# Attention of a decoder trunk: pairs of heads run in common slots, heads side by side in row tiles

## The chip, the cores and the metric

One core of a Trainium2 chip runs the whole kernel. The metric is the device time of one execution, in microseconds; a median stands for the runs shown.

## The reference, cut to what matters

One layer of a decoder trunk on 256 tokens of width 1024, in fp32: a feed-forward with a norm, a mixer with a norm, a second feed-forward with a norm. The mixer runs three causal attentions of six heads each (head width 64) and adds them through sigmoid gates:

```python
x = LN(alpha*x + 0.5*SwiGLU_a(x))
h = x @ w_in                      # q, k, v of three branches, and gates
# MoBA: with 256 tokens and blocks of 256 only the query's own block is left
p = softmax(where(dist >= 0, q k^T / 8 - slope*dist, -inf));  o_m = p v
# differential: two maps of width 32 for each head
w = softmax(s_1) - lam*softmax(s_2);  o = w v
o_d = o * rsqrt(mean(o^2) + eps) * subln_g * (1 - lambda_init)
# stick-breaking: strictly causal
z = q k^T / 8;  log_1m = where(before, log_sigmoid(-z), 0)
tail = cumsum(log_1m, reverse) - log_1m
o_s = where(before, exp(log_sigmoid(z) + tail), 0) v
x = LN(alpha*x + (sum_b sigmoid(g_b + c_b) * (o_b w_br_b)) @ w_out)
x = LN(alpha*x + 0.5*SwiGLU_b(x))
```

## The kernel before

**Big products.** Every weight chunk (128 x 1024) is loaded raw by SP's queue, and then split into a high part, by ACT (L113), and the rest, by DVE (L114), both float32r. A product is made of three: high by high, high by rest, rest by high. `nat_mm` holds the activations and moves 512 weight columns; `trn_mm` holds weight columns and moves 512 and then 256 token columns. Nine split tiles rotate (`HL_BUFS`), and three more where there is room. Products add up in the four PSUM banks of the pool `acc`; the four of `att` serve attention and transposes.

**The order.** The schedule is written by the program itself. Class `Pe` keeps a clock of its own, moved on by each recorded matmul; `pe.later(delay, fn)` queues a piece, and before each product's matmul the pieces that have come due are recorded. So a piece of attention stands wherever that clock reached its time, among the matmuls of a big product, and its ACT and DVE instructions stand at the same place in those engines' rows. `MIX` lists the mixer's products: queries and keys of a pair of heads (`project`), gates in halves (`gates`), branch products (`branch`). Pairs of heads start at least `PACE` = 10 of that clock apart, stick-breaking first (three pairs), then differential, then MoBA.

**Attention of a pair** is in plain fp32, both token tiles at once: 128 columns for the first (only its own keys) and 256 for the second.
- MoBA: `softmax_scores` of each head (two matmuls with 64 rows, at row 0 or 64 of the array); on DVE the bias, the mask and the row's extreme (L574), on ACT the exponential with its sum (L577); `MB_T` later six transposes and two copies on ACT (L585); `MB_O` later `pv` (six matmuls with the transposed map held and 64 value columns moving), a division by the sums on DVE, and `O_M` later `turn_o`, two transposes into `oT`, the form that the branch product needs.
- Differential: two maps of 32 rows for each head. The first head's two maps, then `D_H` later the second's; the combination (L652 to L655) `D_C` after each, the transposes `D_T` after, `pv` at `D_O`, a norm of the output, `turn_o` at `D_F`.
- Stick-breaking: for each head a matmul that writes the mask to a bank over the whole array (`identr` held, `maskr` moving, 384 columns), then the scores onto it (64 rows, heads at row 0 and 64). ACT and DVE make a softplus (L706 to L709) and split it. `ST_T` later the sums (a triangular matrix by both parts) and the carry (`mones`), and an exponential on ACT (L724); `ST_O` later the values, with V held and the map moving, which gives the transposed output at once.

L186 is the one line of all matmuls (`Pe.mm`), L190 that of the transposes (`Pe.tr`).

Of the kernel before, what the change touches and what calls it, by code (L numbers as in the profile page):

```python
# [10 lines left out]
F32 = mybir.dt.float32  # L11
# [5 lines left out]
P = 128  # L17
# [14 lines left out]
# split weight chunks and raw ones held at a time; the first chunks split before the products begin  # L32
# [14 lines left out]
# distances between dependent pieces on TensorE's queue: between pairs of heads, then of the norms' transposes  # L47
# (T), the hidden units' (N), MoBA (MB, O), differential (D) and stick-breaking (ST)
# [102 lines left out]
class Pe:  # L151
    """Matrix products in program order, with a clock by which later pieces are slotted in."""
# [42 lines left out]
def trunk(ctx: ExitStack, tc: tile.TileContext, start_d, x_d, ln_g, ln_b, gu_d, gun_d, down_d, v_d, qk_d, gate_d,  # L195
# [48 lines left out]
    with ExitStack() as es:  # L244
# [10 lines left out]
        # TensorE's clock comes up while the first pieces load  # L255
# [121 lines left out]
    def to_T(src, dst, t, q):  # L377
        """Four 128-column pieces of src (token tile t) transposed and split into dst."""
# [8 lines left out]
    def nat_mm(ps, lhs, k, t, h, l, lo, n, first, last):  # L387
        """One k tile: activations (token tile t) stationary, n weight columns from lo moving."""
# [6 lines left out]
    def trn_mm(ps, src, h, l, k, first, last):  # L395
        """One k tile: 128 weight columns stationary; hi products left, the rest right."""
# [136 lines left out]
    with ExitStack() as es:  # L533
# [6 lines left out]
        # values: the first token tile of two branches first, while the second is normalised  # L540
# [39 lines left out]
        def turn_rows(e):  # L580
# [3 lines left out]
            eT = ep.tile([P, BW], F32, name="eT", bufs=3)  # L584
# [3 lines left out]
        def pv(ps, eT, b, h, r):  # L588
            vc = vcol(b, h)
            o0, o1 = ps[:, r * HD:(r + 1) * HD], ps[:, P + r * HD:P + (r + 1) * HD]  # L590
            pe.mm(o0, eT[:, 0:P], V[:, 0, vc], True, True)
            pe.mm(o1, eT[:, P:S], V[:, 0, vc], True, False)
            pe.mm(o1, eT[:, S:BW], V[:, 1, vc], False, True)

        def turn_o(o, b, p):
            ps = att.tile([P, 512], F32, name="att")
            for t in range(2):
                pe.tr(ps[:, t * P:(t + 1) * P], o[:, t * P:(t + 1) * P], ident)
            act_split(oT[b][:, p, 0:S], oT[b][:, p, S:2 * S], ps[:, 0:S])
            pairs_done[b] += 1  # L600
# [3 lines left out]

        def moba_pair(p, qT, kT):
            sm = small.tile([P, 2, 2], F32, name="sm")
            nmx = small.tile([P, 2, 2], F32, name="nmx")
            es_ = []
            for r in range(2):
                e = ep.tile([P, BW], F32, name="e")  # L610
                softmax_scores(qT, kT, r * 64, 64, SLOPES[2 * (2 * p + r)], e, nmx[:, r, :], sm[:, r, :])
                es_.append(e)
            exps[0] -= 1
            eTs = []

            def values():
                eTs.extend(turn_rows(e) for e in es_)

            def more():
                ps = att.tile([P, 512], F32, name="att")  # L620
                for r in range(2):
                    pv(ps, eTs[r], 0, 2 * p + r, r)
                rs = small.tile([P, 2, 2], F32, name="rsm")
                nc.vector.reciprocal(rs, sm)
                o = ep.tile([P, S], F32, name="s1", bufs=5)
                nc.vector.tensor_tensor(
                    o.rearrange("p (t r c) -> p t r c", t=2, r=2),
                    ps[:, 0:S].rearrange("p (t r c) -> p t r c", t=2, r=2),
                    rs.rearrange("p r t -> p t r").unsqueeze(3).to_broadcast([P, 2, 2, HD]), op=ALU.mult)
                pe.later(O_M, lambda: turn_o(o, 0, p))  # L630
            pe.later(MB_T, values)
            pe.later(MB_O, more)

        def diff_pair(p, qT, kT):
            sm = small.tile([P, 2, 2, 2], F32, name="smd")
            nmx = small.tile([P, 2, 2, 2], F32, name="nmxd")
            ws_ = {}
            eTs = {}

            def head(r):  # L640
                sl = SLOPES[2 * (2 * p + r) + 1]
                ee = []
                for m in range(2):
                    e = ep.tile([P, BW], F32, name="e")
                    softmax_scores(qT, kT, r * 64 + m * 32, 32, sl, e, nmx[:, m, r, :], sm[:, m, r, :])
                    ee.append(e)
                if r:
                    exps[0] -= 1

                def combine():  # L650
                    c = small.tile([P, 2], F32, name="c")
                    nc.vector.reciprocal(c, sm[:, 1, r, :])  # L652
                    nc.vector.scalar_tensor_tensor(c, sm[:, 0, r, :], nlam, c, op0=ALU.mult, op1=ALU.mult)
                    for t, cs in enumerate((slice(0, P), slice(P, BW))):
                        nc.vector.scalar_tensor_tensor(ee[0][:, cs], ee[1][:, cs], c[:, t:t + 1], ee[0][:, cs],  # L655
                                                       op0=ALU.mult, op1=ALU.add)
                    ws_[r] = ee[0]

                def turn():
                    eTs[r] = turn_rows(ws_[r])  # L660
                pe.later(D_C, combine)
                pe.later(D_T, turn)

            def more():
                ps = att.tile([P, 512], F32, name="att")
                for r in range(2):
                    pv(ps, eTs[r], 1, 2 * p + r, r)
                rs = small.tile([P, 2, 2], F32, name="rsm")
                nc.vector.reciprocal(rs, sm[:, 0])
                o = ep.tile([P, S], F32, name="s1", bufs=5)  # L670
# [4 lines left out]
                sq = ep.tile([P, S], F32, name="s1", bufs=5)  # L675
# [5 lines left out]
                nc.gpsimd.tensor_tensor(ms, ms, mhalf[:, 0:4], op=ALU.pow)  # L681

# [5 lines left out]
                pe.later(D_F, lambda: turn_o(o, 1, p))  # L688
            head(0)
            pe.later(D_H, lambda: head(1))  # L690
            pe.later(D_O, more)

        def stick_pair(p, qT, kT):
            zs, sps = [], []
            sh = lnp.tile([P, D], F32R, name="ln_g")
            sl = lnp.tile([P, D], F32R, name="ln_b")
            for r in range(2):
                ps = att.tile([P, 512], F32, name="att")
                rr = slice(r * 64, (r + 1) * 64)
                pe.mm(ps[:, 0:BW], identr, maskr, True, False, skip_group_check=True)  # L700
                pe.mm(ps[:, 0:S], kT[rr, 0:P], qT[rr, 0:S], False, False, tile_position=(r * 64, 0),
                      skip_group_check=True)
# [205 lines left out]
```

## Time and profile before

| | |
|---|---|
| median of 3 runs | 616.0 us (612.36, 616.0, 618.33) |
| span of the profiled execution | 612.6 us |
| mean granted clock of TensorE | 0.997 |
| busy: PE, weight loads | 601.5, 511.3 us |
| busy: DVE, ACT, GpSimd | 406.5, 327.6, 26.9 us |

The profiled execution's span is that from its first to its last instruction; no other time of that execution is given, and the fastest of the three runs is 612.36 us. The mixer with its attention lies between about 223 and 400 us; attention ends at 352.

### The profile page before, as it was taken

How to read it: one execution, taken by the hardware profiler on the slowest of the kernel's cores; microseconds unless marked ns; L12 is line 12 of the kernel's file. 1: busy time of each engine (PE TensorE's matmuls, PEld its weight loads, DVE VectorE, ACT ScalarE, POOL GpSimd, SP SyncE). 2: the span in 40 equal slices, each digit the busy share in tenths (PEclk: the TensorE clock that was granted, in tenths of full speed). 3: DMA queues.
4: the chain of work that ended last, by engine and by line, in shares of the span. 5: the costliest groups of instructions: out<-in, count | busy, mean ns of one | idle time of the engine just before them, and what ended most of it. 6: DMA issues, size and time to landing. Idle time of an engine off the chain costs nothing.

```text
span 612.6 us, 8640 instructions
## 1 busy us (share of the span) xinstructions
PE 601.5 (98%) x3186; PEld 511.3 (83%) x3186; DVE 406.5 (66%) x656; ACT 327.6 (53%) x561; POOL 26.9 (4%) x63
## 2 busy tenths in 40 slices
PE   8999999999999999999999999999999999999995
PEld 7888888888889988878688888888788888888884
DVE  5879767664438666567786586789866676674217
ACT  6868556553312677565647564444755566563200
POOL 1610000000001000000020000001000000000001
PEclk9999999999999999999999999999999999999998
DMA  8899765666531783443444547454965566656001
GB/s 326 288 365 311 261 180 180 191 194 210 155 103 61 259 307 122 150 154 119 139 143 157 173 171 239 138 172 163 321 239 196 185 183 193 201 185 197 1 1 68
DMA packets 32538, 113.35 MB, mean 185 GB/s; under 512 B 3680, under 2 KB 4448, under 8 KB 32496
## 3 DMA queue, kind: packets, MB, share of 16 engines
q1 hardware_dynamic: 30816, 106.97, 52.6%
q0 software_dynamic: 1680, 5.83, 3.0%
q8 instruction: 25, 0.41, 0.3%
q14 instruction: 17, 0.14, 0.1%
HBM read 111.74 MB, written 1.05 MB: 184 GB/s over the span
## 4 chain that ended last, share of the span: by engine, by line
PE 89%; DVE 3%; issue 3%; DMA 3%; ACT 1%; POOL 0%; SPq 0%; DVEq 0%; ACTq 0%; POOLq 0%
PE acc L186 82%; PE att L186 6%; DMA raw<-gu 2%; PE att L190 1%; DMA sraw<-start 1%; DVE wx L114 1%; DVE w L114 1%; ACT wx L113 0%; POOL rs L353 0%; DVE x L362 0%; ACT e L577 0%; DVE x L358 0%; DVE e L574 0%; DVE e L655 0%; ACT w L113 0%
## 5 line engine op out<-in xcount | busy, mean ns | idle before, releaser
L114 DVE TENSOR_TENSOR w<-raw,w 128x1024 fp32r<-128x1024 f32 (+1 forms) x166 | 197.8, 1206 | 76.8 <-ACT w L113 76.0
L186 PE MATMUL acc<-xT,w 128*128 128x512 f32 x1264 | 228.1, 339 | 0.0
L186 PEld LDWEIGHTS acc<-xT,w 128*128 128x128 f32 x1264 | 193.7, 188 | 29.2 <-issue 1.5
L113 ACT ACTIVATE w<-raw 128x1024 fp32r<-128x1024 f32 (+1 forms) x166 | 170.5, 1040 | 83.0 <-PE acc L186 70.4
L186 PE MATMUL acc<-w,xT 128*128 128x512 f32 (+1 forms) x576 | 132.5, 382 | 0.0
L186 PEld LDWEIGHTS acc<-w,xT 128*128 128x128 f32 x576 | 104.4, 188 | 17.0 <-issue 1.0
L186 PE MATMUL acc<-w,hT 128*128 128x512 f32 (+1 forms) x408 | 93.5, 383 | 0.0
L186 PEld LDWEIGHTS acc<-w,hT 128*128 128x128 f32 x408 | 74.9, 188 | 14.9
L465 ACT ACTIVATE lo<-acc 128x256 f32<-128x256 f32 x76 | 27.9, 375 | 60.0 <-PE acc L186 60.0
L467 DVE TENSOR_TENSOR gu<-acc,lo 128x256 f32<-128x256 f32 x76 | 31.3, 419 | 38.7 <-ACT lo L465 38.6
L114 DVE TENSOR_TENSOR wx<-raw,wx 128x1024 fp32r<-128x1024 f32 (+1 forms) x30 | 36.3, 1212 | 12.7 <-ACT wx L113 12.6
L186 PE MATMUL acc<-xT,wx 128*128 128x512 f32 x240 | 43.9, 337 | 0.0
L186 PEld LDWEIGHTS acc<-xT,wx 128*128 128x128 f32 x240 | 36.7, 188 | 5.2
L113 ACT ACTIVATE wx<-raw 128x1024 fp32r<-128x1024 f32 (+1 forms) x30 | 31.3, 1046 | 11.5 <-PE acc L186 10.2
L186 PE MATMUL acc<-wx,hT 128*128 128x512 f32 (+1 forms) x138 | 32.8, 380 | 0.0
L186 PEld LDWEIGHTS acc<-wx,hT 128*128 128x128 f32 x138 | 25.2, 188 | 4.9
L344 DVE SCALAR_TENSOR_TENSOR x<-x,acc 128x512 f32<-128x512 f32 x11 | 7.5, 682 | 28.1 <-PE acc L186 28.1
L186 PE MATMUL acc<-w,oT 128*128 128x512 f32 x108 | 25.6, 392 | 0.0
L353 POOL TENSOR_TENSOR rs<-rs,mhalf 128x1 f32<-128x1 f32 x6 | 5.9, 976 | 406.6 <-DVE rs L352 406.6
L240 ACT ACTIVATE hT<-gu 128x256 fp32r<-128x256 f32 x40 | 16.6, 415 | 13.1 <-DVE gu L472 12.1
L186 PEld LDWEIGHTS acc<-w,oT 128*128 128x128 f32 x108 | 20.1, 188 | 4.0
L471 ACT ACTIVATE gu<-gu 128x256 f32<-128x256 f32 x40 | 16.4, 409 | 2.6 <-DVE gu L467 2.5
(132 smaller groups left out, 411.4 us busy)
## 6 DMA issues: line engine op xcount, KB each, us to landing
raw<-gu SPq DMA_DIRECT2D x76, 512.0 KB, 4.9
raw<-down SPq DMA_DIRECT2D x44, 512.0 KB, 4.1
raw<-gates SPq DMA_DIRECT2D x24, 512.0 KB, 4.2
raw<-qk SPq DMA_DIRECT2D x18, 512.0 KB, 4.4
raw<-v SPq DMA_DIRECT2D x12, 384.0 KB, 3.1
raw<-w_out SPq DMA_DIRECT2D x8, 512.0 KB, 5.1
raw<-gun SPq DMA_DIRECT2D x8, 512.0 KB, 4.9
sraw<-start SPq DMA_DIRECT2D x7, 384.0 KB, 6.1
```

Source lines behind the costliest of these rows:

```text
L113: self.nc.scalar.activation(h[:, :n], raw[:, :n], AF.Copy)
L114: self.nc.vector.tensor_tensor(l[:, :n], raw[:, :n], hv[:, :n], op=ALU.subtract)
L186: self.nc.tensor.matmul(out, lhsT=lhsT, rhs=rhs, start=start, stop=stop, **kw)
L190: self.nc.tensor.transpose(out, in_, ident)
L240: nc.scalar.activation(dst_h, src, AF.Copy)
L344: nc.vector.scalar_tensor_tensor(xs, xs, ALPHA, ps[:, 0:n], op0=ALU.mult, op1=ALU.add)
L353: nc.gpsimd.tensor_tensor(rs, rs, mhalf[:, 0:1], op=ALU.pow)
L465: nc.scalar.activation(lo, ps[:, S:2 * S], AF.Copy)
L467: nc.vector.tensor_tensor(v, ps[:, 0:S], lo, op=ALU.add)
L471: nc.scalar.activation(g, g, AF.Silu)
```

## The change

All pairs that are under way advance together. A pair is now a list of stages, each a table from a kind of piece to a function, and `slot()` takes the next stage of every pair, and runs all pieces of one kind before those of the next, in the order `KINDS`. A new pair enters with each slot, and slots are `PACE` apart. Besides that:
- `scores` records the scores of both heads of a pair, or of the differential pair's four maps, kind by kind, so that neighbours stand in different row tiles. The four maps take two banks from `acc` and two from `att`. Stick's two masks come together, before both heads' scores.
- MoBA normalises the rows of its map on DVE (`M_N` after the scores) ahead of the transposes, and then takes `values_T`, with V held, in place of `pv` and `turn_o`.
- The two combinations of a differential pair come 5 and 7 after the scores (`D_C0`, `D_C1`). The pool of `s1` has 3 tiles for 5, that of `eT` 4 for 3, and a tile `o` is new.

Comments and docstrings go, which shifts line numbers: L186, L190, L113, L114, L574, L577, L585, L655, L724 are L180, L184, L106, L107, L582, L585, L593, L663, L745 after.

```diff
-MB_T = 4.0
-MB_O = 6.0
-O_M = 2.5
-D_H = 4.0
-D_C = 3.5
-D_T = 8.0
-D_O = 14.0
+M_N = 4.0
+D_C0 = 5.0
+D_C1 = 7.0
 D_S = 2.5
-D_F = 7.0
-ST_T = 6.5
-ST_O = 1.5
...
-    def mm(self, out, lhsT, rhs, start, stop, **kw):
+    def mm(self, out, lhsT, rhs, start, stop, share=1, **kw):
...
-        self.t += (n / 2.4 if r else max(4 * n / 2.4, 214)) / 1000
+        self.t += (n / 2.4 if r else max(4 * n / 2.4, 214)) / share / 1000
...
-        def softmax_scores(qT, kT, r0, kk, slope, e, nmx, sm):
-            ps = att.tile([P, 512], F32, name="att")
-            r = slice(r0, r0 + kk)
-            tp = (r0, 0)
-            pe.mm(ps[:, 0:P], qT[r, 0:P], kT[r, 0:P], True, True, tile_position=tp)
-            pe.mm(ps[:, P:BW], qT[r, P:S], kT[r, 0:S], True, True, tile_position=tp)
+        def scores(maps, qT, kT, row_q):
+            st, mv = (qT, kT) if row_q else (kT, qT)
+            first = row_q
+            for kind in range(2):
+                for r0, n, ps in maps:
+                    r, tp = slice(r0, r0 + n), (r0, 0)
...
+                    pe.mm(out, st[r, a], mv[r, b_], first, first, tile_position=tp, share=len(maps),
+                          skip_group_check=not row_q)
...
+        def values_T(b, p, eTs):
+            po = att.tile([P, 512], F32, name="att")
+            for kt, cs, ws in ((0, slice(0, S), slice(0, S)), (1, slice(P, S), slice(S, BW))):
+                for r in range(2):
+                    pe.mm(po[r * HD:(r + 1) * HD, cs], V[:, kt, vcol(b, 2 * p + r)], eTs[r][:, ws], kt == 0, kt == 1,
+                          tile_position=(0, r * 64), share=2, skip_group_check=True)
+            act_split(oT[b][:, p, 0:S], oT[b][:, p, S:2 * S], po[:, 0:S])
             pairs_done[b] += 1
...
+        KINDS = ("sums", "mask", "carry", "turn_o", "pv", "turn", "valT", "scores")
...
+                def norm():
+                    rs = small.tile([P, 2, 2], F32, name="rsm")
+                    nc.vector.reciprocal(rs, sm)
+                    for r in range(2):
+                        for t, cs in enumerate((slice(0, P), slice(P, BW))):
+                            nc.vector.tensor_scalar(es_[r][:, cs], es_[r][:, cs], rs[:, r, t:t + 1], None,
+                                                    op0=ALU.mult)
+                pe.later(M_N, norm)
+
+            return [{"scores": start},
+                    {"turn": lambda: eTs.extend(turn_rows(e) for e in es_)},
+                    {"valT": lambda: values_T(0, p, eTs)}]
...
+                banks = [(acc if i < 2 else att).tile([P, 512], F32, name="acc" if i < 2 else "att")
+                         for i in range(4)]
+                scores([(i * 32, 32, banks[i]) for i in range(4)], qT, kT, True)
...
+                pe.later(D_C0, lambda: combine(0))
+                pe.later(D_C1, lambda: combine(1))
...
+            return [{"scores": start},
+                    {"turn": lambda: eTs.extend(turn_rows(e) for e in ee[::2])},
+                    {"pv": pv},
+                    {"turn_o": turn_o}]
...
+            return [{"mask": mask, "scores": start},
+                    {"sums": sums, "carry": carry},
+                    {"valT": lambda: values_T(2, p, wts)}]
...
+        def slot(new=None):
+            if new is not None:
+                under_way.append(new)
+                begun[0] += 1
+            now = [pair.pop(0) for pair in under_way]
+            for kind in KINDS:
+                for stage in now:
+                    if kind in stage:
+                        stage[kind]()
+            under_way[:] = [pair for pair in under_way if pair]
+            if begun[0] == 3 * NP and under_way:
+                pe.later(PACE, slot)
...
-            def begin():
-                begun[0] += 1
-                attend[b](p, *res)
-            pe.later(at - pe.t, begin)
+            pe.later(at - pe.t, lambda: slot(attend[b](p, *res)))
```

**Where the instructions move.** On PE, the first stick-breaking pair (slot one), inside the next pair's query product: the masks (`maskr`) and the scores (`qT,kT`) of two heads, before.

```order
778 L186 MATMUL att<-maskr,identr 128x384
779 L186 MATMUL att<-qT,kT 128x256
780 L186 MATMUL att<-qT,kT 128x128
781 L186 MATMUL att<-maskr,identr 128x384
782 L186 MATMUL att<-qT,kT 128x256
783 L186 MATMUL att<-qT,kT 128x128
784 L186 MATMUL acc<-xT,w 128x256
```

The same place after:

```order
777 L180 MATMUL acc<-xT,w 128x512
778 L180 MATMUL att<-maskr,identr 128x384 x2
779 L180 MATMUL att<-qT,kT 128x256 x2
780 L180 MATMUL att<-qT,kT 128x128 x2
781 L180 MATMUL acc<-xT,w 128x256
```

The second head's mask no longer stands between the two heads' scores, and both heads' matmuls of one shape are neighbours.

On PE, the first differential pair's scores (`kT,qT`) in a gate product, before: two maps of the first head, the third stick pair's values (`eT,V`), a big product's piece (`acc<-w,xT`), then two maps of the second head, of which the last row is cut off here.

```order
917 L186 MATMUL att<-kT,qT 128x128
918 L186 MATMUL att<-kT,qT 128x256
919 L186 MATMUL att<-kT,qT 128x128
920 L186 MATMUL att<-kT,qT 128x256
921 L186 MATMUL att<-eT,V 64x256
922 L186 MATMUL att<-eT,V 64x128
923 L186 MATMUL att<-eT,V 64x256
924 L186 MATMUL att<-eT,V 64x128
925 L186 MATMUL acc<-w,xT 128x512 x13
926 L186 MATMUL att<-kT,qT 128x128
927 L186 MATMUL att<-kT,qT 128x256
928 L186 MATMUL att<-kT,qT 128x128
```

After, slot four, where the first differential pair starts together with the second stick pair's values (`eT,V`) and the third's sums:

```order
893 L180 MATMUL att<-ln_g,trir 128x384
894 L180 MATMUL att<-ln_b,trir 128x384
895 L180 MATMUL att<-e,mones 128x128 x2
896 L180 MATMUL att<-eT,V 64x256 x2
897 L180 MATMUL att<-eT,V 64x128 x2
898 L180 MATMUL acc<-kT,qT 128x128 x2
899 L180 MATMUL att<-kT,qT 128x128 x2
900 L180 MATMUL acc<-kT,qT 128x256 x2
901 L180 MATMUL att<-kT,qT 128x256 x2
902 L180 MATMUL acc<-w,xT 128x512 x32
```

Four maps stand side by side, two of them in banks of `acc`, and pieces of three pairs form one stretch between two pieces of a big product.

On DVE, between the scores of slot five (the second differential pair's) and the transposes of slot six, after: weight splits (`w<-raw,w`) and the combinations (L659 to L663, reading `c`) of that pair's two heads.

```order
241 L787 SCALAR_TENSOR_TENSOR qT<-acc,qsc,s_2812 128x256
242 L790 TENSOR_TENSOR kT<-acc,s_2833 128x256
243 L107 TENSOR_TENSOR w<-raw,w 128x1024 x2
244 L659 RECIPROCAL c<-smd 128x2
245 L660 SCALAR_TENSOR_TENSOR c<-smd,nlam,c 128x2
246 L663 SCALAR_TENSOR_TENSOR e<-e,c 128x128
247 L663 SCALAR_TENSOR_TENSOR e<-e,c 128x256
248 L107 TENSOR_TENSOR w<-raw,w 128x1024
249 L659 RECIPROCAL c<-smd 128x2
250 L660 SCALAR_TENSOR_TENSOR c<-smd,nlam,c 128x2
251 L663 SCALAR_TENSOR_TENSOR e<-e,c 128x128
252 L663 SCALAR_TENSOR_TENSOR e<-e,c 128x256
```

Before, two heads' combinations in that part of DVE's row, right behind the reading of the later head's scores, with one split between them:

```order
264 L652 RECIPROCAL c<-smd 128x2
265 L653 SCALAR_TENSOR_TENSOR c<-smd,nlam,c 128x2
266 L655 SCALAR_TENSOR_TENSOR e<-e,c 128x128
267 L655 SCALAR_TENSOR_TENSOR e<-e,c 128x256
268 L114 TENSOR_TENSOR w<-raw,w 128x1024
269 L652 RECIPROCAL c<-smd 128x2
270 L653 SCALAR_TENSOR_TENSOR c<-smd,nlam,c 128x2
271 L655 SCALAR_TENSOR_TENSOR e<-e,c 128x128
272 L655 SCALAR_TENSOR_TENSOR e<-e,c 128x256
```

After, the first combination has the evacuation of the next queries and keys and two splits ahead of it, the second one more split, and the second head's transposes on PE stand right behind the first's (row 976 of PE's order after, six in a row, ahead of the third pair's scores). In slots seven and eight the same six transposes are followed at once by MoBA's scores (rows 1023 and 1024, 1072 and 1073); in slot nine two heads' values stand between.

## Rows read from the trace of the kernel before

**Rows 1.** Page of the profile, its part 1: busy time, share, instructions of each engine.

```profile
PE 601.5 (98%) x3186; PEld 511.3 (83%) x3186; DVE 406.5 (66%) x656; ACT 327.6 (53%) x561; POOL 26.9 (4%) x63
```

**Rows 2.** Busy times in three windows; the first line names the columns.

```profile
core 0: us, PE busy (x) PEld busy (x) DVE busy (x) ACT busy (x) POOL busy (x), PEclk, DMA share, GB/s
60.00:110.00 50.00, 50.00 (x285) 43.34 (x284) 34.44 (x56) 29.44 (x56) 0.00 (x0) 1.00 0.68 214
140.00:180.00 40.00, 40.00 (x178) 33.14 (x177) 16.93 (x16) 12.62 (x14) 0.00 (x0) 1.00 0.54 163
223.00:352.00 129.00, 128.01 (x730) 104.26 (x729) 85.42 (x199) 80.10 (x175) 4.13 (x5) 1.00 0.45 148
```

**Rows 3.** Groups of matmuls by form, PE, 223 to 352 us; tile shape, moving shape, count.

```profile
L186 PE MATMUL acc<-w,xT 128*128 128x512 f32 x192 | 49.0, 400 | 0.0
L186 PE MATMUL acc<-xT,w 128*128 128x512 f32 x128 | 45.7, 396 | 0.0
L186 PE MATMUL att<-qT,kT 64*128 64x256 f32 x12 | 4.2, 428 | 0.0
L186 PE MATMUL acc<-w,oT 128*128 128x512 f32 x11 | 2.9, 400 | 0.0
L186 PE MATMUL att<-kT,qT 64*128 64x256 f32 x12 | 1.8, 377 | 0.0
```

**Rows 4.** Chain of waits, 220 to 352 us: start, duration (us), what, instructions.

```profile
224.33 2.23 PE att L186 x10
...
233.87 1.16 PE att L186 x8
...
247.90 0.81 PE att L186 x8
...
271.96 0.86 PE att L186 x8
...
282.54 1.28 PE att L186 x12
...
291.20 0.23 PE att L190 x2
...
301.43 0.09 DVE c L652
...
302.07 0.49 DVE e L655
...
318.69 0.86 PE att L186 x8
...
324.18 0.66 PE att L190 x6
```

**Rows 5.** Waits of PE, 200 to 370 us: total, times, longest (us).

```profile
PE att L190 <- DVE e L655: 0.7, 1, 0.7
```

**Rows 6.** Groups of ACT by form, 220 to 400 us.

```profile
L113 ACT ACTIVATE w<-raw 128x1024 fp32r<-128x1024 f32 x49 | 50.1, 1054 | 23.0 <-PE acc L186 20.7 <-issue 1.2 <-DMA raw<-qk 0.7
L577 ACT ACTIVATE e<-e,nmxd 128x256 f32<-128x256 f32 x12 | 5.9, 495 | 0.0
L585 ACT ACTIVATE eT<-att 128x384 f32<-128x384 f32 x12 | 5.4, 480 | 1.7 <-PE att L190 1.6
L577 ACT ACTIVATE e<-e,nmxd 128x128 f32<-128x128 f32 x12 | 4.7, 395 | 11.4 <-DVE nmxd L574 11.4
L761 ACT ACTIVATE s<-acc,qsc 128x256 f32<-128x256 f32 x9 | 4.2, 462 | 5.9 <-PE acc L186 5.9
```

**Rows 7.** Groups of DVE by form, 220 to 400 us.

```profile
L114 DVE TENSOR_TENSOR w<-raw,w 128x1024 fp32r<-128x1024 f32 x49 | 58.6, 1222 | 24.2 <-ACT w L113 24.0
L574 DVE CUSTOM_DVE_ANT_0 e<-att,base 128x256 f32<-128x256 f32 x18 | 7.5, 419 | 0.0
L574 DVE CUSTOM_DVE_ANT_0 e<-att,base 128x128 f32<-128x128 f32 x18 | 5.1, 285 | 1.5 <-PE att L186 1.5
L762 DVE SCALAR_TENSOR_TENSOR qT<-acc,qsc,s 128x256 f32<-128x256 f32 x9 | 4.3, 481 | 4.6 <-ACT s L761 4.6
L765 DVE TENSOR_TENSOR kT<-acc,s 128x256 f32<-128x256 f32 x9 | 3.8, 422 | 6.4 <-ACT s L764 6.3
```

More of the change, by code (lines that the diff above doesn't have):

```diff
@@ L583, in turn_rows @@
                 pe.tr(ps[:, c * P:(c + 1) * P], e[:, c * P:(c + 1) * P], ident)
-            eT = ep.tile([P, BW], F32, name="eT", bufs=3)
+            eT = ep.tile([P, BW], F32, name="eT", bufs=4)
             nc.scalar.activation(eT, ps[:, :BW], AF.Copy)
             return eT
[L588 to L599, printed above, removed]
+        def values_T(b, p, eTs):
[5 more added lines that the diff above has]
+            act_split(oT[b][:, p, 0:S], oT[b][:, p, S:2 * S], po[:, 0:S])
             pairs_done[b] += 1
@@ L607, in moba_pair, with start @@
             nmx = small.tile([P, 2, 2], F32, name="nmx")
[L608 to L620, printed above, removed]
-                for r in range(2):
[L622 to L632, printed above, removed]
+            es_, eTs = [], []
+            def start():
+                banks = [att.tile([P, 512], F32, name="att") for _ in range(2)]
+                scores([(r * 64, 64, banks[r]) for r in range(2)], qT, kT, True)
+                for r in range(2):
+                    e = ep.tile([P, BW], F32, name="e")
+                    exp_rows(banks[r], SLOPES[2 * (2 * p + r)], e, nmx[:, r, :], sm[:, r, :])
+                    es_.append(e)
+                exps[0] -= 1
+                def norm():
[9 more added lines that the diff above has]
+                    {"valT": lambda: values_T(0, p, eTs)}]
         def diff_pair(p, qT, kT):
@@ L636, in diff_pair, with start, combine @@
             nmx = small.tile([P, 2, 2, 2], F32, name="nmxd")
[L637 to L643, printed above, removed]
+            ee, eTs, os_ = [], [], []
+            def start():
+                banks = [(acc if i < 2 else att).tile([P, 512], F32, name="acc" if i < 2 else "att")
+                         for i in range(4)]
+                scores([(i * 32, 32, banks[i]) for i in range(4)], qT, kT, True)
+                for i in range(4):
+                    r, m = i // 2, i % 2
                     e = ep.tile([P, BW], F32, name="e")
-                    softmax_scores(qT, kT, r * 64 + m * 32, 32, sl, e, nmx[:, m, r, :], sm[:, m, r, :])
+                    exp_rows(banks[i], SLOPES[2 * (2 * p + r) + 1], e, nmx[:, m, r, :], sm[:, m, r, :])
                     ee.append(e)
-                if r:
-                    exps[0] -= 1
-                def combine():
+                exps[0] -= 1
+                def combine(r):
                     c = small.tile([P, 2], F32, name="c")
@@ L674, in more @@
                     rs.rearrange("p r t -> p t r").unsqueeze(3).to_broadcast([P, 2, 2, HD]), op=ALU.mult)
-                sq = ep.tile([P, S], F32, name="s1", bufs=5)
+                sq = ep.tile([P, S], F32, name="s1", bufs=3)
                 nc.vector.tensor_tensor(sq, o, o, op=ALU.mult)
@@ new lines, in turn_o @@
+            def turn_o():
+                ps = att.tile([P, 512], F32, name="att")
+                for t in range(2):
+                    pe.tr(ps[:, t * P:(t + 1) * P], os_[0][:, t * P:(t + 1) * P], ident)
+                act_split(oT[1][:, p, 0:S], oT[1][:, p, S:2 * S], ps[:, 0:S])
+                pairs_done[1] += 1
+            return [{"scores": start},
+                    {"turn": lambda: eTs.extend(turn_rows(e) for e in ee[::2])},
+                    {"pv": pv},
+                    {"turn_o": turn_o}]
@@ new lines, in stick_pair, with mask, start, sums @@
+        def stick_pair(p, qT, kT):
+            zs, sps, wts, split = [], [], [], []
+            def mask():
+                zs.extend(att.tile([P, 512], F32, name="att") for _ in range(2))
+                for ps in zs:
+                    pe.mm(ps[:, 0:BW], identr, maskr, True, False, skip_group_check=True)
+            def start():
+                scores([(r * 64, 64, zs[r]) for r in range(2)], qT, kT, False)
+                sh = lnp.tile([P, D], F32R, name="ln_g")
+                sl = lnp.tile([P, D], F32R, name="ln_b")
+                split.extend((sh, sl))
+                for r in range(2):
+                    ps = zs[r]
+                    a = ep.tile([P, BW], F32, name="e")
+                    nc.scalar.activation(a, ps[:, 0:BW], AF.Abs)
+                    nc.scalar.activation(a, a, AF.Exp, scale=-1.0)
+                    nc.scalar.activation(a, a, AF.Ln, bias=1.0)
+                    nc.vector.scalar_tensor_tensor(a, ps[:, 0:BW], 0.0, a, op0=ALU.max, op1=ALU.add)
+                    sps.append(a)
+                    cs = slice(r * BW, (r + 1) * BW)
+                    act_split(sh[:, cs], sl[:, cs], a)
+            def sums():
+                for r in range(2):
+                    for part in split:
+                        pe.mm(zs[r][:, 0:BW], trir, part[:, r * BW:(r + 1) * BW], False, False,
+                              skip_group_check=True)
+            def carry():
+                for r in range(2):
+                    pe.mm(zs[r][:, P:S], mones, sps[r][:, S:BW], False, True, skip_group_check=True)
+                for r in range(2):
+                    w = ep.tile([P, BW], F32, name="eT", bufs=4)
+                    nc.scalar.activation(w, zs[r][:, 0:BW], AF.Exp)
@@ L756, in project @@
                     trn_mm(ps, xT, h[:, ks], l[:, ks], k, k == 0, k == KT - 1)
-                lo = ep.tile([P, S], F32, name="s1", bufs=5)
+                lo = ep.tile([P, S], F32, name="s1", bufs=3)
                 v = qkp.tile([P, S], F32, name="qk"[n] + "T")
```

74 lines of the change are left out of this document (20 added, 54 removed).

## The prediction

> **What bounds the kernel now.** I read the page's first part first: TensorE (PE) is busy in 601.5 of 612.6 us [rows 1]. Then the windows, to see whether that is work at full rate. In a stretch of the first feed-forward 285 matmuls, half of 512 and half of 256 columns, take 50.00 us without a gap at clock 1.00: 0.351 us for a pair. In a stretch of the down product 178 of 512 columns take 40.00 us, 0.225 each [rows 2]. So the big products run at one price, PE takes its instructions in order, and whatever attention puts into its row of instructions lengthens the program by just what it takes there. The reader should see in the mixer's window, 223 to 352 us, that DVE is busy for 85.42 and ACT for 80.10 of 129.00 us: neither is the bound, but two thirds full engines hand things over late when work comes in bursts.
>
> What attention costs on PE is a subtraction. In that window stand 192 + 11 big products of 512 columns and 128 pairs [rows 3]: 203 x 0.225 + 128 x 0.351 = 45.6 + 44.9 = 90.5 us. The other **38.5 us** of the 129.0 are attention, its interruptions and 0.99 us in which PE idled [rows 2].
>
> The chain of waits gives the pieces [rows 4]. Stick-breaking, a pair of heads: mask and scores 2.23, sums and carry 1.16, values 0.81, together 4.20. Differential: scores 0.86 for a head's two maps, so 1.72, transposes 0.66, values 1.28, turning the output 0.23, together 3.89. MoBA: scores 0.86, then 0.66, 1.28 and 0.23, together 3.03. Three pairs of each are 33.4 us. The remaining 5.1 us are the idle 0.99 and 4.1 us in which PE goes into and out of some 33 stretches of attention, 0.12 us for each.
>
> **Scores side by side.** The best row for this change is already in the kernel before: MoBA's two heads lie in different row tiles and follow each other at once, and their 12 records of 256 columns then count as 1.8 us busy; stick's 12 of the same shape, with the second head's full-array mask between the heads, count as 4.2 [rows 3]. In the chain the same pair of heads takes 0.86 us (MoBA) against 2.23 less two masks (stick) [rows 4]. A mask is 384 columns at the rate of a big product, 384/512 x 0.225 = 0.17 us. So stick's scores cost 2.23 - 0.34 = 1.89 and will cost 0.86: -1.0 a pair, **-3.1 us**. For the differential pair two maps side by side cost 0.86, and four take 1.72 in two groups. No row shows four abreast. Bounds: as long as two (0.86, saves 0.86 a pair) or no gain (0). I take 0.88, since two tiles cost what one does when they are side by side: **-2.5 us**. The Trainium skill, TensorE: Matmul & The Clock Gate (Measured speedup vs the span model), gives 3.07 and not 4 as the speed-up of four row tiles. By that page four maps would take 0.86 x 4/3.07 = 1.12 us, an estimate, and this term would be 0.7 us smaller; no run here shows it.
>
> **MoBA's values.** Transposes stay (0.66). The 1.28 and the 0.23 of turning the output go, and the form of stick's values, 0.81, comes: -0.7 a pair, **-2.1 us**. The normalisation moves ahead of the transposes: a reciprocal and four multiplies on DVE in place of a reciprocal and one. No row has this multiply; the query's scaling of 256 columns takes 0.48 [rows 7], so at most 4 x 0.48 - 0.48 = 1.4 us a pair on DVE, four times in hiding: DVE is idle for 44 of 129 us. It falls in the 10 us between two slots, and I give it 0.2 us in the one slot where little else lies between.
>
> **Fewer interruptions.** Eleven slots instead of 33 stretches, each with 0.1 us out and 0.09 for the change into tile mode: 4.1 becomes 2.1, **-2.0 us**. The idle 0.99 goes with the waits that make it: the longest is 0.7 us of the transposes behind the combination L655 [rows 5]; it is counted again below wherever it comes back.
>
> **The slots without waits**, in order, by the same pieces: mask, scores 1.40; with sums and carry 2.55; with values 3.36; sums, carry, values, four maps 3.05; values, transposes, maps 2.56; pv, transposes, maps 3.03; twice turn, pv, transposes, MoBA scores 3.25; turn, transposes, values, scores 2.75; transposes, values 1.66; values 1.00. The sum is 27.9 us, so 38.5 - 27.9 = **-10.6 us**, within rounding what the four terms and the idle give (3.1 + 2.5 + 2.1 + 2.0 + 1.0).
>
> **What the slots newly wait for.** This is the step against the change. Pieces that were spread over 10 us now stand behind each other, while four `att` banks must be emptied by ACT and DVE.
> - Slot six, second head's transposes: they need combine(1). From the end of slot five's scores the way there is: first map on DVE 0.70, the eight exponentials on ACT 4 x 0.89 = 3.56, the query's two steps 0.46 and 0.48, the key's add 0.42, two weight splits 2.44, combine(0), a split 1.22, combine(1) [rows 6, 7]; a combination takes 1.13, from its first row to the end of its last [rows 4]. Sum 11.5. PE gets there after 8.66 us of big products (the order has 44 between the slots, 25 of pairs and 19 of the gate: 12.5 x 0.351 + 19 x 0.225), 0.1, pv 1.28 and three transposes 0.33: 10.4. With the handovers I take **1.5 us**.
> - Slots seven to nine: MoBA's scores need the bank that the transposes of the same slot have just filled. ACT empties two in 2 x 0.48, and the first began 0.33 before the last transpose ended: 0.63, with handover some 0.8. I take 0.8, 0.9 (with the multiplies) and 0.6 (values between): **2.3 us**.
> - Slots three and five: values and the fourth map take a bank that an ACT copy of 0.48 in the same slot frees: 0.45 and 0.3, **0.75 us**.
> Together **4.5 us**. Bounds: 1.9 if only four copies of 0.48 show; 7.8 if in five slots a weight split of 1.05 [rows 6] stands ahead of the copy and slot six waits for 2.5. I stay between since the order puts a slot's splits mostly behind its copies. Everything that a wait delays, the next product's evacuation included, sits behind PE anyway; the gates' adds on DVE come, in the order, several big products before their banks are needed again, and nine split tiles of weights are kept ahead of the products, so none starves. The branch products hold the last two slots, whose waits lie behind 47 big products each: nothing there. Loads, first and second feed-forward, norms: unchanged, at zero.
>
> **Sum.** -10.6 + 4.5 = -6.1 us. The profiled execution has a span of 612.6, level with the fastest of the three runs (612.36); the median is 616.0. Against its own span that is 606.5, and at the median 616.0 - 6.1 = 609.9, so **610 us**, -1.0%. One per cent, 6.2 us, is about what a measurement of this kernel can tell from no change, and the forecast sits on that bound.
>
> **Rivals.** *A, the waits are small:* ACT's copies come out as fast as PE asks for them and slot six is not late, so 1.9 instead of 4.5: 616 - 8.7 = 607. For it: before, the one wait over 0.2 us in this window is the 0.7 of [rows 5], and the whole window idles 0.99 us. Against: the slots put producer and consumer 0.1 us apart. Chance 0.27.
> *B, four maps only run two by two,* or the two stick heads do not overlap because both add into banks that the mask left open: one term of 2.5 or 3.1 is missing, 616 - 3.3 = 613. For it: no row shows four abreast, nor tiles that accumulate onto a mask. Against: MoBA's rows. Chance 0.18; this is also the case of a change that does not do what it says.
> *C, slower:* the burst of a slot isn't drained when the next dependent piece comes. Its place is slots four to nine; each holds four maps' exponentials, 3.6 us on ACT, or two heads' chain with two splits. If the six slots wait a whole 3.6 us, that is 21.6, and 616 - 10.6 + 21.6 = 627; it decides from 10.6 us of waits, 1.8 a slot. Against: ACT is idle for 49 of 129 us and slots are 10 us apart, three times a burst. The Trainium skill, TensorEngine Tiling (Array Packing), PSUM Bottleneck, states this rule: tiles speed up TensorE and not the emptying of PSUM, which may become the bound. Chance 0.05.
>
> **How the numbers follow.** My sum 0.50, A 0.27, B 0.18, C 0.05. The range takes in A with no wait at all (605.4) and B with its own upper waits: 616 - 10.6 + 2.8 + 7.8 = 616.0; so 604.5 to 616. Faster by over 1%: all of A, a third of my own case, which lies on the bound: 0.44. Within 1%: the rest of mine, B, and the upper half of what remains: 0.51. Slower 0.05.
>
> **What will show it.** In the profile after, PE's attention in the mixer should come in eleven stretches; stick's scores of 256 columns should count as MoBA's do (about 1.8 us for 12), and the four maps' block should take about 0.9 us. The waits of PE should name L663 (combination) in one place with about 1.5 us, and L593 and L745 (ACT copies) in some five with 0.3 to 0.9. I am wrong if the four maps' block takes 1.7, if waits sum to under 2 or over 8 us, or if PE starts waiting for weights (L106, L107), which I put at nothing.

## The result, and the profile after

The changed kernel takes 607.71 us in the median (605.33 to 609.27, 4 runs) against 614.75 us before (612.36 to 618.33, 4 runs): a ratio of **0.9896, 95% interval 0.9858 to 0.9934**, so 4 to 9 us faster. The forecast was 610 us and -1.0%, with a range of 604.5 to 616.

The first part of the page after; it answers to [rows 1]:

```profile
PE 593.8 (98%) x3168; PEld 506.5 (84%) x3168; DVE 407.5 (67%) x665; ACT 328.5 (54%) x561; POOL 26.9 (4%) x63
```

PE is as full as before and does less. The chain of waits of the changed kernel, 215 to 385 us (start, duration in us, what, instructions); its pieces answer to [rows 4]:

```profile
222.31 1.21 PE att L180 x10
...
260.19 1.96 PE att L180 x16
262.14 0.31 PE acc L180 x2
262.45 0.01 PE att L180 x2
...
263.00 0.01 PE att L180 x2
263.01 13.15 PE acc L180 x64
...
289.29 1.14 DVE w L107
...
290.80 0.76 DVE e L663 x2
291.55 0.04 issue
291.60 0.44 PE att L184 x2
...
306.65 0.22 PE att L184 x2
306.87 1.29 PE att L180 x12
308.16 0.35 PE att L184 x3
308.50 0.02 issue
308.53 0.50 ACT eT L593
309.03 0.04 issue
309.07 1.30 PE att L180 x6
310.37 7.84 PE acc L180 x44
...
384.92 0.44 PE att L184 x4
```

From the top: slot one, masks and scores, is 1.21 us where the same ten rows of PE (each of the four scores' matmuls leaves two) took 2.23 [rows 4]. In slot four the four maps stand as short pieces in turn in banks of both pools, from 262.14 to 263.01: 0.87 us for four, which is what two took. In slot six PE's transposes (291.60) stand right behind the second combination (290.80), which stands behind a weight split. In slot seven an ACT copy of a transposed map ends, and then MoBA's scores begin. Attention stands in eleven stretches, as forecast. Stick's scores of 256 columns, 4.2 us in [rows 3], count in the profile after as

```profile
L180 PE MATMUL att<-qT,kT 64*128 64x256 f32 x12 | 2.1, 428 | 0.0
```

where about 1.8 was forecast. The last row of the chain is that of the first transposes of the branches' sum; in the chain of waits of the kernel before it reads

```profile
393.45 0.44 PE att L190 x4
```

So the **mixer's stretch**, from the first mask to these transposes, is 384.92 - 222.31 = 162.61 us, and was 393.45 - 224.33 = 169.12: **-6.5 us**. Every changed instruction lies in it. The profiled spans differ by 7.5 (612.6 and 605.1); the rest lies ahead of the first mask and behind these transposes, in the feed-forwards, whose code is the same. They vary from run to run, as a window of the second feed-forward shows in two runs of the changed kernel itself (columns as in [rows 2]). In the profile after:

```profile
430.00:530.00 100.00, 100.00 (x561) 86.20 (x561) 68.17 (x105) 58.93 (x106) 0.00 (x0) 1.00 0.61 199
```

And in another profile of the same kernel (its second run, below):

```profile
430.00:530.00 100.00, 100.00 (x573) 87.68 (x572) 69.09 (x107) 58.74 (x107) 0.00 (x0) 1.00 0.64 205
```

561 and 573 matmuls in 100 us, PE without a gap and the clock at 1.00 in both: 2% for the same work. In the profiles of the fourteen runs of this document, each feed-forward goes at one of two paces, 0.347 or 0.353 us on average between the starts of one pair (512 and 256 columns) and the next; the first is at the slower pace in seven of them, the second in four. The mixer's stretch instead repeats: 162.61 and 162.60 us in these two runs. So whole times tell kernels apart to some 3 us only, and what follows is read from the stretch. Beside it I give attention's **cost on PE**: for each piece of attention, the time from the start of the big product before it to that of the fourth one after it, less those products at their own price (0.230, 0.117 and 0.227 us in the trace), summed. It is 38.2 us before and 31.6 after.

PE's waits in the changed kernel, 200 to 400 us (total, times, longest, us), which answer to [rows 5]:

```profile
PE att L184 <- DVE e L663: 0.9, 1, 0.9
PE att L180 <- ACT eT L593: 0.5, 2, 0.3
PE att L180 <- ACT eT L745: 0.4, 1, 0.4
```

These are the three lines that were forecast, and no wait for weights (L106, L107) is among them. But ACT's copies show in three places and not in some five, and the list sums to 1.8 us, under the 2 that the prediction named as a sign of being wrong. The view counts only gaps between the modelled ends of matmuls; by cost of the slots the waits are 3.6 us (below).

### The profile page after: what moved, and what is told of

It is laid out like the page before. It is cut to its first block, busy times and chain, and to the rows that moved or that the text cites. A ratio compares the mean times of both kernels' runs of the same rounds, so it can differ in the third digit from the quotient of the medians.

```text
span 605.1 us, 8603 instructions
## 1 busy us (share of the span) xinstructions
PE 593.8 (98%) x3168; PEld 506.5 (84%) x3168; DVE 407.5 (67%) x665; ACT 328.5 (54%) x561; POOL 26.9 (4%) x63
## 4 chain that ended last, share of the span: by engine, by line
PE 95%; DVE 2%; ACT 1%; DMA 1%; issue 1%; SPq 0%; DVEq 0%; ACTq 0%
PE acc L180 89%; PE att L180 4%; PE att L184 2%; DMA sraw<-start 1%; DVE w L107 1%; ACT e L585 1%; ACT w L106 0%; DVE e L663 0%; DVE x L356 0%; ACT eT L593 0%; SPq L244 0%; DVE x L352 0%; DVE w L235 0%; ACT w L234 0%; ACT eT L745 0%
## 5 line engine op out<-in xcount | busy, mean ns | idle before, releaser
L107 DVE TENSOR_TENSOR w<-raw,w 128x1024 fp32r<-128x1024 f32 (+1 forms) x166 | 197.6, 1206 | 75.1 <-ACT w L106 74.9
L180 PE MATMUL acc<-xT,w 128*128 128x512 f32 x1264 | 225.3, 338 | 0.0
L180 PEld LDWEIGHTS acc<-xT,w 128*128 128x128 f32 x1264 | 193.6, 188 | 28.6 <-issue 1.0
L106 ACT ACTIVATE w<-raw 128x1024 fp32r<-128x1024 f32 (+1 forms) x166 | 170.3, 1041 | 80.0 <-PE acc L180 66.4
L180 PE MATMUL acc<-w,xT 128*128 128x512 f32 (+1 forms) x576 | 129.2, 379 | 0.0
L180 PEld LDWEIGHTS acc<-w,xT 128*128 128x128 f32 x576 | 105.2, 188 | 18.0 <-issue 1.0
L180 PE MATMUL acc<-w,hT 128*128 128x512 f32 (+1 forms) x408 | 93.5, 383 | 0.0
L180 PEld LDWEIGHTS acc<-w,hT 128*128 128x128 f32 x408 | 74.9, 188 | 14.9
L107 DVE TENSOR_TENSOR wx<-raw,wx 128x1024 fp32r<-128x1024 f32 (+1 forms) x30 | 36.3, 1212 | 12.0 <-ACT wx L106 12.0
L180 PE MATMUL acc<-xT,wx 128*128 128x512 f32 x240 | 44.0, 338 | 0.0
L180 PEld LDWEIGHTS acc<-xT,wx 128*128 128x128 f32 x240 | 36.7, 188 | 5.4
L106 ACT ACTIVATE wx<-raw 128x1024 fp32r<-128x1024 f32 (+1 forms) x30 | 31.3, 1046 | 10.9 <-PE acc L180 10.4
L180 PE MATMUL acc<-wx,hT 128*128 128x512 f32 (+1 forms) x138 | 32.8, 380 | 0.0
L180 PEld LDWEIGHTS acc<-wx,hT 128*128 128x128 f32 x138 | 25.2, 188 | 4.9
L180 PE MATMUL acc<-w,oT 128*128 128x512 f32 x108 | 26.0, 394 | 0.0
L180 PEld LDWEIGHTS acc<-w,oT 128*128 128x128 f32 x108 | 20.0, 188 | 4.4 <-issue 0.3
```

What stands on the lines that cost most here:

```text
L106: self.nc.scalar.activation(h[:, :n], raw[:, :n], AF.Copy)
L107: self.nc.vector.tensor_tensor(l[:, :n], raw[:, :n], hv[:, :n], op=ALU.subtract)
```

## The experiments

Each median stands beside that of the kernel before, measured with it; the two measures are from the profiled run.

| kernel | median, before | ratio (95%) | mixer's stretch | attention on PE |
|---|---|---|---|---|
| before | | | 169.1 | 38.2 |
| changed | 607.7, 614.8 | 0.9896 (0.9858 to 0.9934) | 162.6 | 31.6 |
| changed again | 605.4, 613.8 | 0.9873 (0.9840 to 0.9906) | 162.6 | 31.6 |
| maps by head | 606.9, 613.4 | 0.9922 (0.9888 to 0.9956) | 162.6 | 31.6 |
| maps apart | 607.2, 613.4 | 0.9912 (0.9865 to 0.9958) | 164.4 | 33.2 |
| mask between | 607.9, 613.4 | 0.9933 (0.9908 to 0.9957) | 165.6 | 34.5 |
| MoBA's pv | 609.2, 613.4 | 0.9937 (0.9905 to 0.9969) | 164.0 | 33.0 |
| slots alone | 613.4, 614.3 | 0.9994 (0.9971 to 1.0016) | 168.7 | 37.6 |
| packing alone | 615.8, 613.8 | 1.0021 (0.9999 to 1.0043) | 170.2 | 39.4 |
| packing with room | 609.7, 613.7 | 0.9931 (0.9908 to 0.9954) | 165.2 | 34.3 |
| MoBA's banks | 604.3, 614.3 | 0.9852 (0.9822 to 0.9883) | 160.9 | 29.8 |
| combination early | 607.7, 614.3 | 0.9901 (0.9868 to 0.9934) | 162.3 | 30.5 |
| all waits | 605.5, 614.3 | 0.9863 (0.9833 to 0.9894) | 160.3 | 28.2 |
| wait not moved | 602.2, 613.8 | 0.9813 (0.9787 to 0.9840) | 159.4 | 28.3 |

**Four maps.** Does it need the recording by kind, and do four tiles run at once?

```diff
-scores([(i * 32, 32, banks[i]) for i in range(4)], qT, kT, True)
+scores([(i * 32, 32, banks[i]) for i in range(2)], qT, kT, True, 4)
+scores([(i * 32, 32, banks[i]) for i in range(2, 4)], qT, kT, True, 4)
```

The added 4 is `share`, which moves the program's own clock on as in the changed kernel, so that nothing else changes place.

> The changed kernel with the four maps of a differential pair recorded head by head (first head's 128 columns twice, its 256 columns twice, then the second head's), still back to back; nothing else moves on any engine. Theory 1, matmuls overlap because they lie in different row tiles, in whatever order they stand: the same time as the changed kernel (607.7), within 0.5 us, and the block of slot four stays at 3.05 us on PE. Theory 2, only neighbours of one size run together, so the recording by kind is what gains: +0.86 us in each of three slots, +2.6, about 610.3.

The same stretch to 0.03 us, and slot four costs 3.06 us (3.05). The first theory holds for the orders that were run: by kind, by head, and, in the kernel before, map by map (0.86 us for two). Then with other pieces between the heads:

```diff
-KINDS = (..., "pv", "turn", "valT", "scores")
+KINDS = (..., "pv", "scores0", "turn", "valT", "scores")   # scores0: the first head's two maps
```

> The changed kernel with the first head's two maps recorded before the transposes and values of the slot, so that a full-array or column-tiled piece stands between the two heads' maps; the order on ACT and DVE is the same. My theory (four abreast cost what two cost): PE's slots four and five take 0.86 us more each (3.05 to 3.9 and 2.64 to 3.5); in slot six the 0.86 us fill the wait for the combination (1.3 us), so the sum is +1.7, about 609.4. Rival (four maps run only two by two): every slot unchanged except slot six, which gets shorter by 0.86: about 606.8.

Slot four goes from 3.05 to 3.90 us, slot five from 2.64 to 3.50, slot six stays at 4.4; the stretch grows by 1.8. Slot four's rows in the chain of waits of this kernel:

```profile
262.36 1.16 PE att L180 x8
263.52 0.85 PE acc L180 x8
264.38 1.66 PE att L180 x16
```

1.16 are sums and carry, 0.85 the first head's maps in `acc`, 1.66 the values (0.81) and the second head's maps, another 0.85. Two maps cost what four do side by side, so the rival with pairs of tiles is out. In the changed kernel itself the term is worth the 1.8 us of two slots: in slot six PE waits for the combination anyway.

**The mask between stick's heads.**

```diff
-for ps in zs:
-    pe.mm(ps[:, 0:BW], identr, maskr, True, False, skip_group_check=True)
 ...
-scores([(r * 64, 64, zs[r]) for r in range(2)], qT, kT, False)
+for r in range(2):
+    pe.mm(zs[r][:, 0:BW], identr, maskr, True, False, skip_group_check=True)
+    scores([(r * 64, 64, zs[r])], qT, kT, False, 2)
```

> The changed kernel with the second head's mask matmul between the two stick-breaking heads' scores, as in the kernel before; nothing else moves. My theory: the full-array mask keeps the heads from running side by side, +1.0 us in each of slots one to three (1.41, 2.58 and 3.80 us become 2.4, 3.6, 4.8), +3.1 in all, about 610.8. Rival (heads that add onto an open bank did not overlap after the change either): no difference, 607.7.

Slot one in this kernel's chain of waits is back at the row of before:

```profile
221.89 2.23 PE att L180 x10
```

Slots one to three cost 2.44, 3.62 and 4.61 us (1.41, 2.58 and 3.80): +1.03, +1.04, and +0.81 in slot three, where the mask fills part of a wait. PE's order of time (start, duration, what) splits the 1.03. Slot one with the mask between:

```profile
221.73 0.33 PE L180 MATMUL att<-maskr,identr 128*128 128x384 f32 x1
221.99 0.92 PE L180 MATMUL att<-qT,kT 64*128 64x256 f32 x4
222.84 0.44 PE L180 MATMUL att<-maskr,identr 128*128 128x384 f32 x1
223.21 0.92 PE L180 MATMUL att<-qT,kT 64*128 64x256 f32 x4
224.05 0.61 PE L180 MATMUL acc<-xT,w 128*128 128x256 f32 x2
```

And in the changed kernel:

```profile
222.15 0.52 PE L180 MATMUL att<-maskr,identr 128*128 128x384 f32 x2
222.59 0.92 PE L180 MATMUL att<-qT,kT 64*128 64x256 f32 x8
223.45 0.62 PE L180 MATMUL acc<-xT,w 128*128 128x256 f32 x2
```

From the start of its scores to that of the next piece one head takes 0.85 us, and both together take 0.86: tiles that add onto an open bank overlap too. From a mask's start to the scores behind it the first kernel has 0.26 and 0.37 us, the changed one 0.44 for both masks. So of the 1.03 us some 0.85 are the overlap, and some 0.18 come with the second mask's standing alone behind tiled matmuls.

**MoBA's values as before** (the functions `pv` and `turn_o` with the division between them, in place of `norm` and `values_T`).

> The changed kernel with MoBA's values as before: six matmuls with the transposed map held, division on DVE, two transposes in a slot of their own; the normalisation of the rows ahead of the transposes is gone. My theory: +0.70 us a pair on PE (1.28 + 0.23 for 0.81), +2.1, and one slot more and a longer bank wait in slot nine, +0.5: about 610.3. Rival (the four multiplies on DVE that the change adds cost as much as the products it saves): no difference, 607.7.

Slots nine to eleven and the added twelfth cost 2.14 us more, which is the 2.1 for the products; the further 0.5 that was expected didn't come. And slot eight falls from 3.93 to 3.22: there MoBA's scores got two other banks of `att`. In the trace they wait on DVE's semaphore, where in the changed kernel they wait on ACT's, and no wait shows. So +1.4, by +2.1 for the products and -0.7 for the banks.

**Slots alone**: these three edits (maps apart, mask between, MoBA's pv) at once.

> The slots without any packing: the changed kernel with all three edits of the earlier runs at once (a mask between stick's heads, the differential heads' maps apart, MoBA's values as before). If the terms add, attention costs PE 31.6 + 1.7 + 2.9 + 1.4 = 37.5 us, against 38.2 before, so about 613.6. Theory 1, fewer interruptions give some 3 us and the slots' waits take them back: within 1 us of the kernel before. Theory 2, the slots carry the gain: 610 or less. Theory 3, the slots lose: over 616.

The cost adds as expected, to 37.6 us, and the stretch is 0.4 us under the one of before: the first theory. Running the pairs in slots is worth next to nothing by itself.

**Packing alone**, in the kernel before: both masks ahead of both heads' scores, and MoBA with `norm` 3 after the scores, the transposes at 4 and the values with V held at 6, as in its own order.

> The kernel before with two of the packings and no slots: both of stick's masks ahead of the scores of both heads, and MoBA's rows normalised ahead of the transposes with the values taken with V held. My theory: packing carries the gain without slots: 3 x 1.0 for stick, 3 x 0.7 and three stretches fewer (0.4) for MoBA, so attention costs PE about 32.8 us and not 38.2, -5.4, about 609. Rival (it is the slots that make it pay, as pieces alone wait or overlap poorly): less than half of that.

This expectation failed. Stick's part came (1.41 for 2.44 us in each pair), MoBA's didn't. PE's waits in this kernel:

```profile
PE att L190 <- DVE e L624: 4.6, 3, 3.0
```

L624 is the rows' multiply. In the chain of waits it is seen why it is late:

```profile
333.92 1.28 DVE w L117
335.19 0.10 DVE rsm L621
...
335.31 0.30 DVE e L624
...
335.75 1.07 PE att L190 x6
```

On DVE a weight split (1.28) stands ahead of the reciprocal and the multiplies, and PE's transposes are recorded 1 unit of the program's clock behind them. The three groups of transposes cost 2.29, 4.08 and 1.54 us in place of 0.67: 5.9 us of waits. The last run moves the transposes to 8 and the values to 10:

```diff
-MB_T = 4.0
-MB_O = 6.0
+MB_T = 8.0
+MB_O = 10.0
```

> The run with packing alone, with MoBA's transposes 8 and its values 10 after the scores in place of 4 and 6, so that the rows' normalisation on DVE has room before the transposes; still no slots. My theory: the 5.9 us of waits in front of MoBA's three transposes came from that distance alone; they go, attention costs PE 33.4 us (39.4 - 5.9), the stretch from the first mask to the branch outputs' transposes falls from 170.2 to 164.3 us (169.1 in the kernel before), and the total is about 609. Rival (without slots the normalisation is always late, whatever the distance): waits of over 2 us stay, 612 or more.

No wait on L624 is left, and the stretch falls by 5.0 us, 0.9 less than forecast. The last values have a new wait, 0.7 in the list and 1.2 by their cost (2.18 us for 1.03):

```profile
PE att L186 <- ACT eT L585: 0.7, 1, 0.7
```

So two of the three packings give 3.9 of the 6.5 us without slots, given room, and two numbers of the old schedule give that room as well. Whether the third, four maps side by side, pays without slots was not run; with slots it is worth 1.8.

**The waits of the slots**, taken away by what makes them.

```diff
-banks = [att.tile([P, 512], F32, name="att") for _ in range(2)]    # moba_pair
+banks = [acc.tile([P, 512], F32, name="acc") for _ in range(2)]
```

> The changed kernel with MoBA's two score banks from the pool of the big products in place of the pool of attention. My theory: slots seven to nine wait because the scores need the banks that ACT is still copying the transposes from; 3.93, 3.93 and 3.11 us become 3.27, 3.27 and 2.74, so -1.7 us, about 606.0, and no wait on an ACT copy of a transposed map is left. Rival (the wait is for something else, or the big products then wait for a bank of theirs): no change or slower.

Slots seven to nine cost 3.23, 3.24 and 2.75 us, the stretch is 1.7 shorter, and no wait on L593 is left. The theory holds.

```diff
-D_C1 = 7.0
+D_C1 = 5.5
```

> The changed kernel with the second combination due at 5.5 and not at 7 after the scores, which on DVE puts one weight split behind it in place of ahead of it, nothing else. My theory: the combination ends one split, 1.22 us, earlier, so slot six falls from 4.42 to 3.2 us on PE: -1.2, about 606.5. Rival (the wait for the combination is set by ACT's exponentials, not by DVE's queue): slot six stays over 4 us.

Slot six falls to 3.34 us (4.42), as DVE's queue would have it, but the stretch only by 0.3. PE's waits in this kernel show a new one:

```profile
PE acc L180 <- DVE G L825: 0.6, 1, 0.6
```

And its chain of waits shows where it comes from:

```profile
302.42 0.09 DVE c L659
...
303.05 0.48 DVE e L663
303.53 1.14 DVE w L107
304.67 0.61 DVE G L825
305.28 0.04 issue
305.32 1.56 PE acc L180 x7
```

The third pair's second combination now stands ahead of a split and a gate's add on DVE, and a big product waits for that add's bank.

```diff
-KINDS = (..., "turn", "valT", "scores")
+KINDS = (..., "turn", "scores", "valT")    # with both edits above
```

> Both of these, and stick's and MoBA's values after the scores of a slot, so that slot three's values don't wait for the exponential of the same slot. If the waits are what I think, every slot falls to its pieces: 1.42, 2.56, 3.37, 3.05, 2.56, 3.08, 3.27, 3.27, 2.74, 1.66, 1.01, together 28.0 us against 31.6 in the changed kernel, so -3.5 us, about 604.2. Rival: the waits move to the next piece in the slot, less than half of that comes.

Attention costs 28.2 us, so the slots' waits are what they were taken for (-3.4 of -3.5), but the stretch only falls by 2.3, with the wait on the gate's add in it. At last the early combination for the second pair alone:

```diff
-pe.later(D_C1, lambda: combine(1))    # D_C1 = 7.0 again
+pe.later(5.5 if p == 1 else D_C1, lambda: combine(1))
```

> As the run with all the waits taken away, but only the second differential pair's second combination comes early (5.5); the others stay at 7. The early one of the third pair had put a gate's add on DVE behind a combination that itself waits for ACT, and PE then waited 0.6 us for the bank of that add. My theory: that wait goes, slot six stays at 3.3 us, and the stretch from the first mask to the branch outputs' transposes falls from 160.3 to about 159.5 us (162.6 in the changed kernel, 169.1 before); total about 604. Rival (PE waits there for something else): still 160.3 with a wait on the gate's add.

159.43 us: the expectation to 0.1, with no wait of PE left in the list from 200 to 400 us. At 602.2 us, 0.9813 of before, this version beats both kernels; the changed kernel, measured again beside it, has 605.4.

For that second measurement of the changed kernel this was expected:

> The changed kernel itself again, beside the versions above. Its mixer, from the first mask to the branch outputs' transposes, should repeat within 0.1 us (162.6), while the whole time varies by some 4 us through the two feed-forwards, which are the same in all kernels.

It did repeat (162.60).

## Why the prediction was right, step by step

**The bound.** PE in order, all products at one price, so the sum is what attention takes on PE. It holds: in the mixer the stretch moved by -6.5 us, as attention's cost on PE did by -6.6. I had 38.5 for the cost before by subtraction, and it is 38.2 by the matmuls' own starts. The price of a pair is not the reason, since the mixer's own (0.227, and 0.347 for a pair) give 38.5 again; the 0.3 stays open.

**Terms.** Stick's scores -3.1: +2.9 when undone, 1.03 a pair where no wait covers it. I gave all of it to the overlap; some 0.18 of it is the mask's place, so the size is right and the reason right to five sixths. Four maps -2.5: 0.85 in each of the two slots where it could be seen, 0.87 us for the block where I took 0.88; the third slot's share is hidden by a wait. The Trainium skill, TensorE: Matmul & The Clock Gate (Measured speedup vs the span model), gives 3.07 for four row tiles, there with 512 columns; by that the block would have been 1.12, an estimate. The measurement decides: 0.87 here, with 128 and 256 columns, and four tiles cost what two do. MoBA's values -2.1: 2.14 us when undone. All slots without waits 27.9: 28.2 to 28.3 in the two runs without them.

**Interruptions, -2.0.** Right as an account (slots without waits come out as summed, with this term in it), but as a gain of the slots it is given back: slots alone win 0.4 us of stretch. That they lose in waits within a slot what they save in interruptions and old waits fits this; the two were not measured apart.

**Waits, 4.5.** This is the term that was mis-sized, by 0.9. By the cost of the slots less their cost in the runs without the wait or their pieces: slot six 1.3 (forecast 1.5), seven and eight 0.7 each (0.8, 0.9), nine 0.4 (0.6), three 0.4 (0.45), five 0.1 (0.3), together 3.6. Slot six's 1.3 is against the sum of its pieces; the early combination took 1.1 of it away. The places and releasers were right but for slot five, whose 0.1 is too small to tell. By the letter of the prediction (waits that sum to under 2) the list's 1.8 says wrong: the list was the wrong measure for that sign, since of the waits on L593 it shows 0.5 us where the slots cost 1.7 us more. The norm's multiplies were hidden, at 0.35 and 0.28 us each by the groups of DVE of the changed kernel, 220 to 400 us:

```profile
L633 DVE TENSOR_SCALAR e<-e,rsm 128x256 f32<-128x256 f32 x6 | 2.1, 348 | 0.0
L633 DVE TENSOR_SCALAR e<-e,rsm 128x128 f32<-128x128 f32 x6 | 1.7, 284 | 0.1
```

**Sum.** -6.1 forecast, -6.5 in the stretch, -7.0 in the medians of whole times, whose interval is 4 to 9. Part of the closeness is luck: the slots without waits brought -10.0 for -10.6, the waits cost 3.6 for 4.5, and the two errors point in opposite ways. The 610 us itself stands on a median before of 616.0 from three runs; on the 614.75 of four it would be 608.7. Whether the change is over or under 1% the interval does not decide.

**Rivals.** Small waits (1.9, 607 us): by the time alone, 607.7, this rival is as good as the forecast. The slots' costs decide: 3.6 were measured, nearer to 4.5 than to 1.9. Pairs of tiles: excluded by the 0.85 above. The slower side, that a burst isn't drained: no slot waited over 1.3 us. The emptying of banks did cost 1.7 us in slots seven to nine, which went with other banks. A burst that isn't drained exists too: packing alone, with the same multiplies 1 unit ahead of the transposes, lost 5.9 us on three pieces, to DVE, and ended not faster than before.

## What to carry to other kernels

On a saturated in-order engine, sum the pieces that change and then walk each new neighbourhood for the bank or the operand that the next piece needs; here the first gave -10.6 us where the runs without waits show -10.0, and the second found all five places that cost 0.35 us or more. Matmuls in disjoint row tiles overlapped here in every order tried, with 0.87 us for four maps and 0.86 for two heads, as long as no full-array instruction stood between them; so look for that one and move it. A wait removed by moving work on another engine's queue has to be followed to what now stands behind: an earlier combination saved 1.1 us in its slot and cost most of it at a gate's add, until only the one that was late was moved.

## What I had not expected

Two runs of one program differ by 2% in the rate of the feed-forwards' matmul pairs, with PE full and the clock at 1.00 (561 and 573 in 100 us), while the mixer repeats to 0.1 us in the two profiles of the changed kernel. What sets the pace stays open: no run here was made to find it. And an edit elsewhere can give the same tiles other banks: MoBA's old values, put back, removed a wait of 0.7 us in slot eight that has nothing to do with them.
